# A fused convolution and max pool: moving two of the first loads to ScalarE's DMA queue

## The chip, the core and the metric

The kernel runs on one core of a Trainium2 chip. The core's engines run side by side, each through its own list of instructions: TensorE (PE; its weight loads are listed as PEld), VectorE (DVE), ScalarE (ACT), GpSimd (POOL) and SyncE (SP). Data comes from and goes to the chip's main memory through DMA transfers, which SyncE, ScalarE or GpSimd issue, each on a queue of its own, and which 16 DMA engines carry out. The metric is the time of one execution on the device, in microseconds (us); lower is better.

## The reference

```python
x_pad = np.pad(x, ((0, 0), (0, 0), (pad, pad), (pad, pad)), mode='constant')
conv[b, co] += weight[co, ci, kh, kw] * x_pad[b, ci, kh:kh+h, kw:kw+w]     # over b, co, ci, kh, kw
...
output[b, c, i, j] = np.max(conv[b, c, i*pool_size:(i+1)*pool_size,
                                      j*pool_size:(j+1)*pool_size])
```

`x` is 16 images of 64 channels and 64 x 64 points in f32, `weight` is 128 x 64 x 3 x 3 in f32, and `pool_size` is 2. The output is 16 x 128 x 32 x 32 in f32: a 3 x 3 convolution with a border of zeros, and then the maximum of each 2 x 2 square.

## The kernel before

**Tiles and steps.** Two images of 64 channels fill the 128 partitions, so there are eight pairs of images. Each pair is cut into four chunks of 16 rows of the convolution (eight of the output), which makes 32 steps. A step is of kind K or W (`TYPES`): for K the rows go into TensorE as they are, cast to bf16 (`kx`); for W, sums and differences of neighbouring rows are formed first, from rows kept in f32 (`wx`). The first steps are 0 (K), 1 (W), 2 (K), 3 and 4 (W). `chunk` (L91) says which rows a step needs, `rows_of` (L88) gives them in main memory.

**The first loads (L114 to L129).** In the text of the kernel they stand in this order, all on SyncE's queue: the weights `wraw` (L115, 288 KB), the first nine rows of the first K chunk into `kfirst` (L119, 288 KB), its other eight rows (L120, 256 KB), the second K chunk into `ksecond` (L126, 512 KB), and the first W chunk in two parts (`wload`, L112, 320 KB and 256 KB). All are f32. Later K chunks are loaded by GpSimd's queue, which casts them to bf16 on the way (`kload`, L101); later W chunks by SyncE's queue (L112). Nearly all stores go through SyncE's queue (L485), the last one half through ScalarE's (L487).

**The order of work.** The schedule is written by hand: `ORDER` lists steps by name, and each engine runs its own instructions in that order; a wait is set where data is needed. It begins:

```python
g0 D2 TD2 XOa g2 GS TG0 VD2 D0 XOb XEb TG2 g1 F.0.0 F.0.1 TD0 uG1 GM VG0 GP XEa F.1.0 F.1.1 VD0 F.2.0
uGM EV.0.1 TG1 F.2.1 uGP LB.3 VG2 LK.0.0 TGM X1 LB.4 F.3.0 TGP X2 KS.0 L.11 PA1.2.0 LB.6 Ea F.3.1 VGM
```

- The weights: `g0` (ScalarE, L194), `g1` and `g2` (VectorE, L192) cast the taps, `D2` and `D0` (VectorE, L507 and L508) and `GM` (VectorE, L200) form differences, `GS` and `GP` (GpSimd, L509 and L198) sums. A `T` step turns a block by TensorE (`turn`, L170), a `V` step copies the turned block to where TensorE takes it as weights (`turn_out`; VectorE L188 for D2, D0 and G2, ScalarE L182 and L184 for the others).
- The first K chunk: `XOa`, `XEa` (odd and even rows of the first half of `kfirst`) and `XOb`, `XEb` (the second half) are casts on ScalarE (`cast_rows`, L492). `F.k.0` and `F.k.1` are the products of the two halves (`first_product`, matmuls at L219). F.0 uses the odd rows and the block D2, F.1 the block G0 (`VG0`).
- The second K chunk: `X1` and `X2` cast `ksecond` on ScalarE (`cast_more`, L501).
- `EV` copies a result out on ScalarE (L439), `KS` sums rows on VectorE (L320), `Ea` and `Eb` are row differences of the first W chunk on VectorE (L393).
- `LB.3`, `LB.4`, `LB.6` and so on are later W loads (`late_load`). They wait for the last VectorE step that stands ahead of them in `ORDER`; `L.11` is a W load without that wait. SyncE issues its transfers in order, so a load that waits holds up those behind it.

Before anything is loaded, TensorE runs eight matmuls on ones (L595), and ScalarE loads its table of functions, which is its first instruction and is listed under L194.

Of the kernel before, what the change touches and what calls it, by code (L numbers as in the profile page):

```python
# [11 lines left out]
def kernel(  # L12
# [9 lines left out]
    nc = tc.nc  # L22
# [65 lines left out]
    def rows_of(p, lo, hi):  # L88
        return x[2 * p : 2 * p + 2].rearrange("b c h w -> (b c) h w")[:, lo:hi, :]

    def chunk(q):  # L91
        return (2 * R * q + (q > 0), min(H, 2 * R * (q + 1) + 1))
# [10 lines left out]
    def wload(s, part=None):  # L103
        p, q = place[s]
        lo, hi = chunk(q)
        if s == WSTEPS[0] and q > 0:
            lo = 2 * R * q - 1
        if part == 0:
            hi = 2 * R * q + R + 1
        elif part == 1:  # L110
            lo = 2 * R * q + R + 1
        return nc.sync.dma_start(out=wx[p % NWX][:, lo + 1 : hi + 1, :], in_=rows_of(p, lo, hi))  # L112
# [3 lines left out]
    _, khi = chunk(0)  # L116
    kmid = R + 1
    kfirst = const.tile([128, khi, W], FP32)
    nc.sync.dma_start(out=kfirst[:, 0:kmid, :], in_=rows_of(0, 0, kmid))  # L119
    nc.sync.dma_start(out=kfirst[:, kmid:khi, :], in_=rows_of(0, kmid, khi))  # L120
    klo2, khi2 = chunk(1)
    ksecond = const.tile([128, khi2 - klo2, W], FP32)
    first_loads = (2, 1,)
    for s in first_loads:
        if s == KSTEPS[1]:
            nc.sync.dma_start(out=ksecond, in_=rows_of(0, klo2, khi2))  # L126
        else:
            wload(s, 0)
            wload(s, 1)  # L129
# [508 lines left out]
```

## Time and profile before

| what | value |
|---|---|
| median of 3 runs | 104.94 us (104.35 to 105.64) |
| the profiled execution: its time | 104.47 us |
| the profiled execution: its span | 102.7 us |
| busy: PE, DVE, ACT, POOL | 94%, 89%, 83%, 76% of the span |
| moved by DMA | 23.60 MB, mean 230 GB/s |
| share of the span in the chain that ended last: PE | 88% |
| share of the span in that chain: the load of `kfirst` | 4.2% |

The span runs from the first to the last instruction that the profile shows; the time of the run is 1.8 us longer. Times in the profile count from the start of the span. L12 is line 12 of the kernel. The chain that ended last is followed back from the last instruction, at each step to what released it. "From issue to landing" of a DMA runs from the start of its issue to the last of its completions; each of the 16 DMA engines sends a completion of its own for its eight of the 128 rows of a load. The trace also has every packet that a DMA engine moved, with its queue, start, length and size; here a packet is one partition's row of a load (2304 bytes of `wraw` and of the first half of `kfirst`, 2048 of its second half, 4096 of `ksecond`).

### The profile page before, as it was taken

The numbers are of one execution on the slowest core, as the hardware profiler recorded it, in microseconds if no ns is written. First come the engines' busy times: TensorE is split into PE (matmuls) and PEld (weight loads), VectorE is DVE, ScalarE is ACT, GpSimd is POOL, SyncE is SP. The second block draws the span as 40 slices with busy tenths as digits, with TensorE's granted clock in tenths as the row PEclk, the third lists the DMA queues.
The fourth block names the chain that finished last, engine by engine and source line by source line (L and its number), as shares of the span: only waits on it lengthen the run. The fifth ranks groups of instructions, "written<-read, shape, count | busy, mean of one in ns | idle before, by whom it ended". The sixth has DMA issues, their size and how long they took to land.

```text
span 102.7 us, 2522 instructions
## 1 busy us (share of the span) xinstructions
PE 96.2 (94%) x905; PEld 54.3 (53%) x905; DVE 91.6 (89%) x176; ACT 85.5 (83%) x192; POOL 77.9 (76%) x66
## 2 busy tenths in 40 slices
PE   6969999999999999999999999999999999999920
PEld 2355465444454447655655555567657765555500
DVE  1576979999999999999999989999999999899960
ACT  4278697999889999997998899897989899897830
POOL 6262889995998799489959999789999688990000
PEclk9999999999999999999999999999999999999999
DMA  2989999999999999600538989930803673386553
GB/s 53 286 295 333 281 325 360 362 421 410 293 311 410 311 308 396 220 6 0 175 57 119 245 259 404 389 111 0 307 3 112 216 165 113 106 295 222 208 192 114
DMA packets 13341, 23.60 MB, mean 230 GB/s; under 512 B 1040, under 2 KB 9360, under 8 KB 13328
## 3 DMA queue, kind: packets, MB, share of 16 engines
q1 hardware_dynamic: 12464, 21.20, 58.8%
q0 software_dynamic: 720, 2.10, 11.6%
q8 instruction: 7, 0.11, 0.5%
q10 hardware_dynamic: 144, 0.13, 0.4%
q14 instruction: 6, 0.05, 0.1%
HBM read 17.14 MB, written 8.39 MB: 249 GB/s over the span
## 4 chain that ended last, share of the span: by engine, by line
PE 88%; DMA 4%; DVE 2%; SPq 1%; issue 1%; ACT 0%; DVEq 0%
PE acc L219 86%; DMA kfirst<-in_x_dram 4%; DVE o L477 1%; PE acc L170 1%; DVE acc L467 1%; PE acc L460 1%; SPq L119 0%; ACT kx L492 0%; SPq L115 0%; DVEq L633 0%
## 5 line engine op out<-in xcount | busy, mean ns | idle before, releaser
L219 PEld LDWEIGHTS <-wt 64*128 64x128 bf16 x870 | 51.7, 94 | 39.0 <-issue 2.0
L219 PE MATMUL acc<-wd,wt 64*128 64x504 bf16 (+3 forms) x276 | 54.4, 367 | 0.0
L381 POOL TENSOR_TENSOR wd<-wx 128x1024 bf16<-128x1024 f32 x21 | 49.2, 2360 | 4.5 <-DVE ws L360 2.0
L219 PE MATMUL acc<-kx,wt 64*128 64x504 bf16 (+6 forms) x264 | 44.7, 355 | 0.9 <-DVE wq L508 0.7
L467 DVE TENSOR_TENSOR acc<-acc,ev 128x512 f32<-128x512 f32 x64 | 42.0, 691 | 1.2 <-ACT ev L441 0.7
L219 PE MATMUL acc<-we,wt 64*128 64x512 bf16 (+3 forms) x138 | 32.5, 367 | 0.0
L219 PE MATMUL acc<-ws,wt 64*128 64x512 bf16 (+1 forms) x132 | 32.5, 377 | 0.0
L441 ACT ACTIVATE ev<-acc 128x512 f32<-128x512 f32 x44 | 26.3, 614 | 1.8 <-PE acc L219 1.3
L451 ACT COPY acc<-acc 128x512 f32<-128x512 f32 x42 | 24.5, 591 | 3.0 <-PE acc L219 1.8
L477 DVE TENSOR_TENSOR o<-acc,od 128x256 f32<-128x256 f32 x64 | 24.7, 416 | 0.9 <-ACT od L471 0.9
L471 ACT COPY od<-acc 128x256 f32<-128x256 f32 x64 | 22.8, 382 | 2.2 <-PE acc L219 1.7
L372 POOL TENSOR_TENSOR we<-wx 128x512 bf16<-128x512 f32 x16 | 20.1, 1272 | 4.0 <-PE acc L219 2.4
L219 PE MATMUL acc<-ks,wt 64*128 64x504 bf16 (+1 forms) x60 | 13.7, 377 | 0.0
L439 ACT COPY ev<-acc 128x512 f32<-128x512 f32 x20 | 11.7, 593 | 1.3 <-PE acc L219 1.2
L352 DVE TENSOR_REDUCE ws<-wx 128x512 bf16<-128x1024 f32 x9 | 11.1, 1232 | 0.0
L360 DVE TENSOR_TENSOR ws<-wx 128x512 bf16<-128x512 f32 x7 | 5.3, 766 | 0.0
L320 DVE TENSOR_TENSOR ks<-kx 128x512 bf16<-128x512 bf16 x10 | 4.3, 435 | 0.0
L408 POOL TENSOR_TENSOR wd<-wx 128x512 bf16<-128x512 f32 x2 | 2.5, 1264 | 2.2 <-DVE we L393 2.2
L339 DVE TENSOR_TENSOR ws<-wx,acc 128x512 bf16<-128x512 f32 x6 | 4.1, 675 | 0.0
L595 PE MATMUL acc<-const-bfloat16-1.0 128*128 128x512 bf16 x8 | 3.3, 582 | 0.8 <-PEq L619 0.8
L335 ACT COPY acc<-wx 128x512 f32<-128x512 f32 x6 | 3.6, 598 | 0.1
L372 DVE TENSOR_TENSOR we<-wx 128x512 bf16<-128x512 f32 x4 | 2.9, 749 | 0.3 <-DMA wx<-in_x_dram 0.3
(33 smaller groups left out, 26.6 us busy)
## 6 DMA issues: line engine op xcount, KB each, us to landing
out_dram<-o SPq DMA_DIRECT2D x31, 256.0 KB, 2.9
wx<-in_x_dram SPq DMA_DIRECT2D x10, 512.0 KB, 10.6
wx<-in_x_dram SPq DMA_DIRECT2D x6, 480.0 KB, 9.7
wx<-in_x_dram SPq DMA_DIRECT2D x5, 544.0 KB, 8.5
kx<-in_x_dram POOLq DMA_DIRECT2D x2, 528.0 KB, 7.5
ksecond<-in_x_dram SPq DMA_DIRECT2D x1, 512.0 KB, 6.4
kx<-in_x_dram POOLq DMA_DIRECT2D x1, 496.0 KB, 8.1
wx<-in_x_dram SPq DMA_DIRECT2D x1, 320.0 KB, 6.7
```

Of the source, the lines that this page charges most:

```text
L219: nc.tensor.matmul(acc[t][:, i0:i1, o0:o1], wt[lo : lo + CI, tap_of(m0, kw, h), :], rows(lo, i0, i1, c0, c1), start=start and kw == 1, sto ...
L320: nc.vector.tensor_tensor(out=row["ks", s], in0=t[:, f : f + 2 * R : 2, :], in1=t[:, f + 1 : f + 2 * R : 2, :], op=ADD)
L352: nc.vector.tensor_reduce(out=row["ws", s], in_=t[:, f : f + 2 * R, :].rearrange("p (r two) w -> p r w two", two=2), axis=mybir.AxisListTy ...
L360: nc.vector.tensor_tensor(out=row["ws", s], in0=t[:, f : f + 2 * R : 2, :], in1=t[:, f + 1 : f + 2 * R : 2, :], op=ADD)
L372: inst = (nc.vector if vector else nc.gpsimd).tensor_tensor(out=row["we", s], in0=t[:, f : f + 2 * R : 2, :], in1=t[:, f + 1 : f + 2 * R : ...
L381: nc.gpsimd.tensor_tensor(out=row["wd", s], in0=t[:, f + 1 : f + 1 + 2 * R, :], in1=t[:, f - 1 : f - 1 + 2 * R, :], op=SUB)
L439: nc.scalar.copy(out=ev[s, h], in_=acc[t])
L441: nc.scalar.mul(ev[s, h], acc[t], -1.0)
L451: nc.scalar.copy(out=acc[t], in_=acc[ta[s, h]])
L467: nc.vector.tensor_tensor(out=t, in0=t, in1=ev[s, h], op=MAX)
L471: nc.scalar.copy(out=od[s, h], in_=acc[tb[s, h]][:, :, 1::2])
L477: nc.vector.tensor_tensor(out=ot[s][:, h], in0=acc[t][:, :, 0::2], in1=od[s, h], op=MAX)
```

## The change

Two of the first loads are issued by ScalarE in place of SyncE: the first nine rows of the first K chunk (L119) and the second K chunk (L126). The weights, the rest of the first K chunk (L120) and the first W chunk stay on SyncE's queue.

```diff
     kfirst = const.tile([128, khi, W], FP32)
-    nc.sync.dma_start(out=kfirst[:, 0:kmid, :], in_=rows_of(0, 0, kmid))
+    nc.scalar.dma_start(out=kfirst[:, 0:kmid, :], in_=rows_of(0, 0, kmid))
     nc.sync.dma_start(out=kfirst[:, kmid:khi, :], in_=rows_of(0, kmid, khi))
...
         if s == KSTEPS[1]:
-            nc.sync.dma_start(out=ksecond, in_=rows_of(0, klo2, khi2))
+            nc.scalar.dma_start(out=ksecond, in_=rows_of(0, klo2, khi2))
```

In the lists of instructions that come out, ScalarE issues the two loads first, ahead of its table load; SyncE issues `wraw`, the second half of `kfirst` and the two parts of the first W chunk one after the other. The lists of PE, VectorE and GpSimd are the same in both kernels.

## The prediction

> **What bounds the kernel now.** I read the chain of waits first, because it tells which stretch the end hangs on.
>
> ```profile
> 0.74 0.38 SPq L115
> ...
> 1.18 0.42 SPq L119
> ...
> 1.65 4.30 DMA kfirst<-in_x_dram
> ...
> 5.98 0.41 ACT kx L492
> ...
> 6.43 0.50 PE acc L219 x6
> 6.93 0.33 PE acc L170 x4
> ...
> 12.27 84.18 PE acc L219 x785
> ```
>
> Columns are start, length (us), work. The start hangs on a load: the second half of the first K chunk (L120; call it *b*, the first half L119 *a*) is issued at 1.65 and lands at 5.95; ScalarE casts it (XOb), the second product F.0.1 runs, then TensorE works without a break. The table by stages, cut at the ends of that last row, says whether a late start is made good:
>
> ```profile
> 12.27:96.45 84.18, 84.18 (x794) 48.27 (x795) 81.82 (x154) 76.37 (x172) 71.62 (x42) 1.00 0.72 234
> ```
>
> First PE busy, then PEld, DVE, ACT, POOL, granted clock, DMA share, GB/s. PE is busy 84.18 of 84.18 us: no gap to catch up in. A delay of F.0.1 passes to the end one for one. So the question is when *b* lands. The timeline shows the engines around that:
>
> ```profile
> 3.59 0.53 ACT L194 CAST wq<-wraw 128x192 bf16<-128x192 f32 x1 [1.57 <-DMA wraw<-in_weight_dram]
> ...
> 5.31 0.41 ACT L492 CAST kx<-kfirst 128x256 bf16<-128x256 f32 x1 [1.19 <-DMA kfirst<-in_x_dram]
> ...
> 5.76 0.50 PE L219 MATMUL acc<-kx,wt 64*128 64x256 bf16 x6 [0.70 <-DVE wq L508]
> ...
> 5.98 0.71 ACT L492 CAST kx<-kfirst 128x256 bf16<-128x256 f32 x2 [0.26 <-DMA kfirst<-in_x_dram]
> ...
> 6.43 0.50 PE L219 MATMUL acc<-kx,wt 64*128 64x256 bf16 x6 [0.16 <-ACT kx L492]
> ...
> 8.51 1.14 ACT L501 CAST kx<-ksecond 128x512 bf16<-128x512 f32 x2
> ```
>
> The idle time ahead of a piece and what ended it stand in brackets. By these starts and the loads' completions, weights land at 3.57, *a* at 5.29, *b* at 5.95, ksecond (*ks*) at 8.49 (its cast starts at 8.51). The DMA view of two windows tells how busy the engines are, and how two queues share them:
>
> ```profile
> DMA packets 1103, 2.89 MB, mean 289 GB/s; under 512 B 115, under 2 KB 115, under 8 KB 1103
> ...
> q1 hardware_dynamic: 1101, 2.89, 91.9%
> ```
>
> ```profile
> q1 hardware_dynamic: 84, 0.32, 55.5%
> q0 software_dynamic: 69, 0.14, 48.1%
> ```
>
> The first is 2 to 12 us: SyncE's queue alone holds the 16 engines 92% of the time, so these loads are bound by data, not by issue. The second is 13 to 14.5 us, with a GpSimd load (q0) and SyncE loads (q1) in flight together: packets 69 to 84, time 48% to 55%. Two queues get about equal turns. The packet records of single engines show turns of one packet, mostly q1, q0, q1, q0: the GpSimd load's eight packets on an engine, 0.172 us each (1.4 in all), need about 2.5 us (first packet 11.95, first completion 14.41).
>
> **The change part by part.** *a* and *ks* leave SyncE's queue for ScalarE's; nothing else moves, and the orders on PE, DVE and POOL stay.
>
> SyncE: two issues go. Rows of 0.42 (L119) and 0.43 (L126) with gaps of 0.05 put *b* at 1.18 in place of 1.65 and the two first wx loads at 1.65 and 2.11 in place of 2.59 and 3.05. Value: nothing, because data is the limit; the ends are 0 and 0.47 us of gain for *b*. The Trainium skill, "DMA: Bandwidth & Descriptors", section "Issuing engines are not separate DMA queues", says that issuing from several engines saves only sequencer time, since all share the same 16 engines. By it the gain is at most that 0.47, and the rows agree.
>
> ScalarE: two issues come first, each between 0.37 (its own issue at the end, L487) and 0.70 (GpSimd's, L101). With 0.47 a piece the table load (1.28) moves from 0.74 to 1.68 and ends at 2.96; with 0.70, at 3.42. Both lie ahead of its next work, which waited 1.57 us for the weights until 3.59. Cost 0; the cover is the wait for weights, which here gets longer.
>
> Weights against *a*: a 2304-byte packet takes 0.093 us, and each engine has 8 of each load. Before, the weights went first; now both queues start together and alternate, so the weights end about where *a* ended: all but one engine had finished *a* by 4.45, the last by 5.29. The weights are then late by 0.9 to 1.7. Cover: D2, g2, VD2 and D0 on DVE follow the weights and D0 ended at 5.75, so they end at 6.65 to 7.45; F.0.0 (needs VD2, which ended at 5.08) can start at 6.0 to 6.8. If F.0.1 stayed at 6.43, up to 0.4 of this would show; if *b* is over 1 us late, all is hidden. *a* itself: 0 (the same work is ahead of it).
>
> *b* against *ks*: this is the cost. Before, an engine did weights, *a*, *b*, then *ks*. Now *b* follows the weights in one queue, *ks* follows *a* in the other, and they alternate: 8 packets of 0.084 (0.67 us) between 8 of 0.159 (1.27 us). Ends: at best nothing gets ahead of *b* and its earlier issue counts, -0.47; without any stall, 4.45 + 0.67 + 1.27 = 6.39, +0.44; if *ks* goes wholly first, *b* lands where *ks* did, 8.49, +2.54. I take a value near the last: the work of an engine up to the end of *b* and *ks* together is what it was, stalls included (eleven packets of *ks* took 0.5 to 1.2 us in place of 0.159), and in turns of one the last packet of *b* is one packet of *ks* ahead of the end: 8.49 - 0.16 = 8.33, less about another packet if SyncE's queue has the lead: 8.2. Delay of *b*: 8.2 - 5.95 = 2.25 us.
>
> *ks* ends where it did (8.2 to 8.5). Its casts stand behind EV.0.1, which now starts near 10.3: covered, 0. The first wx loads come behind the same bytes as before: 0; DVE's first wx product at 9.32 served a matmul at 10.91, now near 13.2.
>
> Queued behind XOb on ScalarE: XEb, VG0, XEa, EV.0.1; F.1.0 needs VG0, so F.1.0 goes from 7.22 to 9.5. On SyncE, the late load LB.3 waits for GM on DVE (3.1 us in the waits; GM follows the weights), so it issues 0.9 to 1.7 after 6.6; behind it LB.4 and L.11. LB.3 landed at 13.2 for a DVE difference that TensorE took at 14.83; TensorE is now 2.25 later, so that is covered too. On POOL, the kx load at 7.62 moves as the weights do; its data is needed after 18.
>
> Sum: 0 + 0 + 0 (weights, under *b*) + 2.25 (*b*) = 2.25 us. Profiled execution: span 102.7, its time 104.47, so 104.47 + 2.25 = 106.7. The median of the runs shown, 104.94, is 0.47 above the profiled run; by it the same sum gives 107.2.
>
> **The rivals.** (1) *Turns of a whole load, not of a packet, SyncE first.* Then an engine does weights, *a*, *b*, *ks* as before and the queue change does nothing: 104.5 to 105.2, say 104.7. This is the rival on the other side (not slower); it decides if *b* is served at most one packet of *ks* later. For it: stores of the tail, on both hardware queues, run in stretches of up to eight packets of one queue; against it, those reached the engines at different times, and at 12 to 14 us q1 gave way after single packets. The Trainium skill, same page, section "Queues, rings and completion order", says that an engine round-robins between queue rows a packet at a time, typically 9 to 17 descriptors, which would be all of one load's share of an engine. By that rule the time would be this rival's; the packet records of 13 to 14.5 us speak against it.
>
> (2) *Faster:* *b* lands early behind the weights alone. TensorE's idle times of 0.70 and 0.16 ahead of F.0.0 and F.0.1 are what could go: 104.47 - 0.86 = 103.6. It needs the weights not to be late, and both queues to outrun one; the 92% says there is little room.
>
> (3) *The clock falls.* TensorE would idle from 4.05 to near 8.6 but for 0.8 us of transposes and 0.5 of F.0.0. The warm-up matmuls ran at 3.27/8 = 0.41 us each, half of the later rate (0.215 a start), and full clock is granted from 3.6 us on; if it falls, some 3.3 us of matmuls again run at half rate, +1.7: 108.4. For it, the thinner work; against it, the clock after the last matmul (about 97.8) falls only at 102.6, some 5 us later, and the gap between 5.07 and 5.76 cost nothing. The Trainium skill, "TensorE: Matmul & The Clock Gate", Part 1, puts the fall behind an idle window of about 3.4 us; by it the gap of 1.4 to 2.2 us between F.0.0 and F.0.1 leaves the clock up.
>
> **How the numbers follow.** Turns of one packet, 0.60: 106.7, own range 105.9 to 107.4 (*b* between 7.4 and 8.5 with other stalls, plus the 0.47). Rival 1, 0.20: 104.7. Rival 2, 0.05: 103.6. Rival 3, 0.15: 108.4. The range 104.6 to 108.0 leaves out rival 2, a quarter of rival 1 and two thirds of rival 3: 0.05 + 0.05 + 0.10 = 0.20. Two per cent, about what a measurement of this kernel can tell from no change, is 2.1 us: 107.04 against 104.94. Slower: 0.42 of the first case (0.25) and rival 3 (0.15), 0.40. Faster: 0.03 (most of rival 2 stays under 2%, 102.8). Same: 0.57.
>
> **What would show it.** Right: in the chain the kfirst DMA ends near 8.2, XOb starts there, F.0.1 near 8.6, and PE is then unbroken for the same length; weights land at 4.4 to 5.3; the ACT queue's packets hold about half of the engines from 2 to 8 us. Wrong: kfirst's second half landing before 6.4 (rival 1), PE's matmuls of 8 to 12 us taking twice their length (rival 3), the weights landing after 6 so that D0, not XOb, gates TD0, or a wait inside the stretch of 84 us.

## The result, and the profile after

| | before | changed |
|---|---|---|
| median of 20 runs each | 105.03 us | 106.13 us |
| lowest to highest | 104.26 to 107.18 | 104.94 to 106.61 |
| the profiled execution | 104.47 | 106.61 |
| its span | 102.7 | 104.8 |

The ratio of the changed kernel to the kernel before is 1.0088, with a 95% interval of 1.0059 to 1.0118: slower, by about 0.9%, and within the 2%. Ratios leave out runs over 1.5% above a kernel's fastest; here their records point to TensorE's clock, which is part of the question (below), so medians over all runs stand beside the ratios. The changed kernel's 20 runs fall into two groups, 6 at 104.94 to 105.14 and 14 at 105.97 to 106.61; the profiled run is one of the second.

The chain of waits of the changed kernel (start, length, work):

```profile
0.74 4.37 DMA wraw<-in_weight_dram
...
5.13 0.51 DVE wq L507
...
5.78 0.40 PE acc L170 x4
...
6.20 0.44 DVE wt L188
...
6.68 1.21 PE acc L219 x12
7.89 0.54 PE acc L170 x4
8.43 1.88 PE acc L219 x18
...
14.43 84.19 PE acc L219 x785
```

The chain now starts from the weights, not from `kfirst`: they land at 5.11 in place of 3.57, and D2, its turn, its copy out and the first products follow one another with waits of at most 0.14 us. The long stretch of TensorE is as long as before (84.19 against 84.18 us), and it starts 2.16 us later (14.43 against 12.27). That is the whole loss of the profiled run: 106.61 - 104.47 = 2.14.

The changed kernel's timeline:

```profile
0.74 0.40 ACTq L119 DMA_DIRECT2D kfirst<-in_x_dram  x1
...
1.65 1.28 ACT L194 ACT_TABLE_LOAD   x1 [1.65 <-PEq L619]
...
5.13 0.50 DVE L507 TENSOR_TENSOR wq<-wraw 128x192 bf16<-128x192 f32 x1 [4.00 <-DMA wraw<-in_weight_dram]
...
5.78 0.83 PE L170 MATMUL acc<-ident,wq 128*128 128x128 bf16 x12 [1.61 <-DVE wq L507]
...
6.68 1.21 PE L219 MATMUL acc<-kx,wt 64*128 64x256 bf16 x12
6.68 0.71 ACT L492 CAST kx<-kfirst 128x256 bf16<-128x256 f32 x2 [0.71 <-DMA kfirst<-in_x_dram]
...
8.36 1.94 PE L219 MATMUL acc<-kx,wt 64*128 64x192 bf16 x18
```

The second half of `kfirst` is late too (6.66 against 5.95, where XOb starts at 6.68). F.0.0 and F.0.1 stand in one row of 12 matmuls, which hides a second wait. By the trace's records of single instructions XOb ends at 7.08 and F.0.1 starts at 7.14, the same 0.05 us behind XOb as before (6.38 and 6.43); at the pace of F.0.0, two matmuls each 0.11 us, it could have started at 7.02. So F.0.1 is 0.70 us late by way of *b*, and would have been 0.59 late by the weights alone. TensorE waits 1.61 us for the weights. And the 18 matmuls of F.1 and F.2.0 take 1.94 us. The same 18 before:

```profile
7.22 1.08 PE L219 MATMUL acc<-kx,wt 64*128 64x192 bf16 x18
```

The table by stages of the changed kernel tells why (PE, PEld, DVE, ACT, POOL busy, then granted clock, DMA share, GB/s):

```profile
4.00:6.00 2.00, 0.39 (x6) 0.26 (x6) 0.87 (x2) 0.84 (x2) 0.00 (x0) 1.00 1.00 376
6.00:8.00 2.00, 1.93 (x25) 1.19 (x23) 1.84 (x5) 1.32 (x4) 1.04 (x2) 0.81 0.93 364
8.00:10.00 2.00, 2.00 (x22) 1.36 (x20) 1.53 (x5) 0.54 (x2) 1.86 (x5) 0.50 0.39 108
10.00:12.00 2.00, 2.00 (x25) 1.00 (x21) 0.65 (x2) 1.84 (x5) 0.00 (x0) 0.83 0.96 234
```

From 4 to 6 us TensorE has 0.39 us of work; from 8 to 10 the granted clock is 0.50, where it was 1.00 before. Its records put the half clock at 7.25 to 10.66. PE shows as fully busy there: a matmul at half clock is just longer, so the clock column and the length of one matmul have to be read beside the busy time.

How the two queues share, 1.5 to 6 us:

```profile
q1 hardware_dynamic: 285, 0.56, 46.7%
q10 hardware_dynamic: 237, 0.68, 41.3%
```

Packets, MB, share of the 16 engines: SyncE's queue (q1) and ScalarE's (q10) get about equal turns.

So the theory after the profile: **(weights)** the nine rows of `kfirst` are asked for at the same instant as the weights and no longer behind them, the weights land 1.5 us later, and TensorE starts late; **(clock)** the longer idle time lets the clock fall, or come late, in some runs. Rivals: ksecond's turns ahead of the second half of `kfirst` (the prediction's own step), or a loss from using two queues at all.

### The profile page after: what moved, and what is told of

Same layout as the page of the kernel before. It is cut to its first block, busy times and chain, and to the rows that moved or that the text cites. A ratio compares the mean times of both kernels' runs of the same rounds, so it can differ in the third digit from the quotient of the medians.

```text
span 104.8 us, 2522 instructions
## 1 busy us (share of the span) xinstructions
PE 97.7 (93%) x905; PEld 54.9 (52%) x905; DVE 91.5 (87%) x176; ACT 85.5 (82%) x192; POOL 78.0 (74%) x66
## 4 chain that ended last, share of the span: by engine, by line
PE 88%; DMA 4%; DVE 3%; issue 1%; DVEq 0%
PE acc L219 86%; DMA wraw<-in_weight_dram 4%; PE acc L170 2%; DVE o L477 1%; DVE acc L467 1%; PE acc L460 1%; DVE wq L507 0%; DVE wt L188 0%; DVEq L633 0%
## 5 line engine op out<-in xcount | busy, mean ns | idle before, releaser
L219 PE MATMUL acc<-kx,wt 64*128 64x504 bf16 (+6 forms) x264 | 45.8, 366 | 0.1
L170 PE MATMUL acc<-ident,wq 128*128 128x128 bf16 x25 | 2.6, 244 | 1.6 <-DVE wq L507 1.6
L507 DVE TENSOR_TENSOR wq<-wraw 128x192 bf16<-128x192 f32 x1 | 0.5, 498 | 4.0 <-DMA wraw<-in_weight_dram 4.0
```

The source lines that it names most:

```text
L170: nc.tensor.transpose(tp[:, (j - lo) * CO : (j - lo + 1) * CO], wq[:, j : j + 2, :].rearrange("a b c -> a (b c)"), ident,)
L219: nc.tensor.matmul(acc[t][:, i0:i1, o0:o1], wt[lo : lo + CI, tap_of(m0, kw, h), :], rows(lo, i0, i1, c0, c1), start=start and kw == 1, sto ...
```

## The experiments

Twelve kernels, each timed against the kernel before on the same chip.

| run | median, us | before, same chip | ratio (95% interval) |
|---|---|---|---|
| e1 nine rows alone on ScalarE's queue | 106.22 | 105.03 | 1.0122 (1.0095 to 1.0149) |
| e2 ksecond alone | 106.84 | 105.03 | 1.0178 (1.0151 to 1.0205) |
| e3 changed, 14 warm-up matmuls | 105.16 | 105.03 | 1.0033 (1.0014 to 1.0051) |
| e4 changed, a copy ahead | 105.45 | 105.03 | 1.0051 (1.0030 to 1.0071) |
| e5 before, idle gap filled | 105.27 | 105.23 | 1.0013 (0.9985 to 1.0042) |
| e6 loads wait for the table | 109.92 | 105.23 | 1.0426 (1.0371 to 1.0481) |
| e7 e1 with 14 warm-up matmuls | 105.37 | 105.23 | 1.0029 (0.9997 to 1.0061) |
| e8 one queue, weights second | 105.05 | 105.23 | 1.0037 (0.9999 to 1.0074) |
| e9 e2 with 14 warm-up matmuls | 105.67 | 105.21 | 1.0047 (1.0026 to 1.0068) |
| e10 before, 4 warm-up matmuls | 106.61 | 105.21 | 1.0041 (0.9988 to 1.0094) |
| e11 changed, weights lead by 0.43 us | 104.92 | 105.06 | 1.0003 (0.9987 to 1.0019) |
| e12 e1, weights lead by 0.43 us | 104.74 | 105.06 | 0.9990 (0.9960 to 1.0020) |

**One part of the change alone.** e1 moves L119 only, e2 L126 only.

```diff
-    nc.sync.dma_start(out=kfirst[:, 0:kmid, :], in_=rows_of(0, 0, kmid))
+    nc.scalar.dma_start(out=kfirst[:, 0:kmid, :], in_=rows_of(0, 0, kmid))
```

> Only the first nine rows of kfirst go to ScalarE's queue; ksecond is back on SyncE's, behind the second half of kfirst. Theory (weights): the weights share the engines with those nine rows as in the changed kernel, land near 5.1, and the first product starts at about 6.7 behind them; the time stays at that of the changed kernel, ratio to before 1.007 to 1.013. Rival (ksecond): the delay comes from ksecond getting turns ahead of the second half of kfirst; then that half lands at 6.0 or sooner, and the ratio is 0.997 to 1.003.

In e1 the weights land at 4.58, sooner than the forecast 5.1, and the second half of `kfirst` at 5.63, sooner than before (5.95); yet the ratio is 1.0122. So the loss does not need ksecond ahead of `kfirst`. F.0.0 starts at 6.62, as forecast, but for another reason: full clock came only at 8.98 in this profile, and the 12 transposes ahead of F.0.0 take 1.44 us in place of 0.83.

> Only ksecond goes to ScalarE's queue; weights and both halves of kfirst stay on SyncE's in their old order. Theory (weights): the weights now take turns with ksecond's 4096-byte packets, so they land at 4.5 to 5.2 in place of 3.6, and both halves of kfirst come later too (second half 6.5 to 7.5); ratio 1.005 to 1.015. Rival (the nine rows): only what ScalarE's queue takes ahead of the weights at the very start matters, and ksecond, which is asked for at the same instant, does no harm: ratio 0.997 to 1.003.

In e2 the weights land at 5.24, just past the forecast, and the second half of `kfirst` at 7.13, within it; the ratio, 1.0178, is above the forecast. Whether 4096-byte packets of ksecond delay the weights more than the 2304-byte ones of the nine rows is not shown: 5.24 is later than e1's 4.58, but close to the changed kernel's 5.11. The forecast missed the clock, which in this profile came only at 10.07.

**The clock.** e3 adds six matmuls to the eight of the warm-up.

```diff
-    for n in range(8):
+    for n in (0, 1, 2, 3, 4, 5, 6, 7) + (7,) * 6:
```

> The changed kernel with six more of the 512-column matmuls on ones behind the eight that are there (14 in all); they fill the time in which TensorE waits for the weights. Theory (clock): of the changed kernel's loss in the profiled execution 1.2 us is TensorE at half clock between 7.3 and 10.7, and its runs near 106.2 are those with such a stretch; with TensorE kept busy that stretch goes, nearly all runs fall near 105.0 to 105.3, ratio 0.999 to 1.004. Rival (loads alone): the spread is due to when the loads land; the added matmuls change nothing or cost up to 0.5 us, ratio 1.007 to 1.014.

The weights land at 4.86, hardly sooner than in the changed kernel, but all 12 runs lie at 104.99 to 105.72: the group near 106.2 is gone. e3's chain of waits:

```profile
0.78 5.03 PE acc L595 x14
...
6.55 0.50 PE acc L219 x6
7.05 0.03 issue
7.08 0.51 PE acc L219 x6
...
7.92 1.04 PE acc L219 x18
...
12.92 84.19 PE acc L219 x785
```

The 18 matmuls take 1.04 us again. e7 and e9 do the same to e1 and e2.

> Only the nine first rows on ScalarE's queue, and six more warm-up matmuls (14 in all). Theory (late weights and, through them, the clock): with the clock kept up only the weights' lateness is left, about 1 us of which the first product's old wait for the nine rows hides some; ratio 1.000 to 1.005, and the difference to the same kernel without the six matmuls is over 0.7 us. Rival (loads alone): ratio 1.008 to 1.014, as without them.

> Only ksecond on ScalarE's queue, and six more warm-up matmuls (14 in all). Without them the ratio was 1.0178, with the clock granted only at 10.1 in the profile. Theory (loads and clock, each with its share): the loads land as there (weights near 5.2, second half of kfirst near 7.1), so F.0.1 starts near 7.6 in place of 6.43, and with the full clock granted by 6 the ratio falls to 1.006 to 1.013. Rival (loads alone): it stays at 1.015 to 1.020. Rival (clock alone): 0.999 to 1.004.

e7 fell from 1.0122 to 1.0029 and e9 from 1.0178 to 1.0047, with the loads of e1 and e2 (weights at 4.85 and 5.46). e9 is below the theory's range and its interval reaches into that of the clock alone: about three quarters of e2's loss was the clock, (178 - 47)/178.

What is left in e3 and e9 goes by way of *b* in their profiles. It lands at 6.60 and 7.04, F.0.1 starts 0.05 us behind the end of XOb (at 7.08 and 7.52), and the long stretch starts 0.65 and 1.09 us later than before, as much as *b* is late (5.95 before). In e7 *b* is on time (5.55), and its chain hangs on the 14 warm-up matmuls themselves, which end at 6.40; what is left there is no measure of the loads.

e10 asks the opposite: the kernel before, all its loads as they were, with less warm-up.

```diff
-    for n in range(8):
+    for n in range(4):
```

> The kernel before with four warm-up matmuls in place of eight; loads, queues and all other work as before. Theory (clock): with TensorE idle from 2.5 to 4.2 the full clock is granted a window of 3.4 us later, near 7 to 10, and the matmuls up to then take twice as long: +0.8 to +2.0 us, ratio 1.008 to 1.019, the weights still landing near 3.6. Rival (loads alone): the loads land as before, ratio 0.997 to 1.003.

Eight of its 12 runs are at 106.2 to 108.3, and four at 105.06 to 105.33, as if nothing had been taken away; the median is 1.4 us above that of the kernel before (1.3%, within the forecast, while the ratio, 1.0041, is not). So the clock can cost as much as the change without any load being moved. Its profiled run is no clean case: the weights landed at 3.57, but the two halves of `kfirst` at 6.47 and 7.18. Its timeline shows the matmuls at half speed all the same (the first row is the kernel before, the second e10):

```profile
4.24 0.83 PE L170 MATMUL acc<-ident,wq 128*128 128x128 bf16 x12 [0.19 <-DVE wq L507]
4.24 1.44 PE L170 MATMUL acc<-ident,wq 128*128 128x128 bf16 x12 [1.60 <-DVE wq L507]
```

The clock column says 1.00 there; in this trace its first record is at 10.12, and what lies ahead of the first record counts as full. The length of the matmul is the better witness.

e5 fills the idle 0.7 us of the kernel before with three matmuls behind the transposes (`WU` in `ORDER`, behind TG2).

> The kernel before with three 512-column matmuls on ones more, in TensorE's idle 0.7 us ahead of the first product; loads as before. Theory (clock): some of the kernel's own runs, those of 106.8 to 107.4, are runs in which the full clock was granted late; with the gap filled these go, the median is 104.7 to 105.0, ratio 0.996 to 1.002, and no run is over 106. Rival: such runs have another cause; they stay, and the added matmuls cost up to 0.5 us.

The ratio is that of no change. One of its 12 runs is over 106, and six of 29 of the kernel before on that chip are over 106.5. The mean granted clock that is listed with each run says what such runs are. In the four timings of the kernel before beside these experiments, 20 of 94 runs are over 106, all with a mean of 0.980 or less; the other 74, none over 105.70, have 0.986 or more. So the kernel before has runs with more half clock too. No run of e5 is below 0.988: in favour of the theory, but with 12 runs not enough to call it shown that the filled gap keeps them away.

In the changed kernel two of the 14 runs of the upper group have 0.974, the profiled one among them, and twelve have 0.987 to 1.000. A clock that comes late leaves no mark in that figure: e1's profiled run has 1.000. So in most of these runs the clock probably came late, and the profile shows the rarer case, in which it fell again.

**The weights' lead.** e4 was to hold back ScalarE's loads by a one-column copy ahead of them.

> The changed kernel with a one-column copy on ScalarE ahead of its two loads, so that the table load comes first and the two loads are issued near 2.1 and 2.6 in place of 0.7 and 1.2. Theory (weights): the weights land near 3.6 again, both halves of kfirst by 5.3, the first product starts near 5.6; ratio 0.994 to 1.002. Rival (two queues as such): sharing between the queues slows the start whichever load is ahead; kfirst's halves land after 6.3, ratio 1.004 to 1.015.

It did not: the load was issued at 0.80 beside the table load, which ran from 0.73 to 2.01; ScalarE's queue did not wait for it. The weights land at 5.11, F.0.0 starts at 6.68, both as in the changed kernel. That makes the two profiles a close pair, since here the clock stayed up. e4's stage table:

```profile
6.00:8.00 2.00, 1.93 (x31) 1.36 (x30) 1.84 (x5) 1.42 (x4) 1.03 (x2) 1.00 0.96 381
8.00:10.00 2.00, 2.00 (x32) 1.13 (x30) 1.55 (x5) 1.51 (x4) 2.00 (x5) 1.00 0.50 161
```

Its long stretch starts at 12.99. Against 12.27 before, 0.72 us is what late loads cost in these profiles; from 12.99 to 14.43 in the changed kernel, 1.44 us, is the clock. Why it stayed up is open: TensorE has 1.72 us of work from 3.85 to 7.26 in e4 and the same 1.72 from 3.84 to 7.25 in the changed kernel, and the clock fell only behind the second. Seven of e4's eight runs lie at 105.28 to 105.53, but only six of the 20 of the changed kernel in its lower group, so chance from run to run may not be all of it.

e6 makes the loads wait for a copy into `kfirst` itself, behind the table load.

> The changed kernel, but ScalarE's two loads wait for a one-column copy into kfirst, which ScalarE does behind its table load; they are issued near 2.2 and 2.7 in place of 0.7 and 1.2. Theory (weights): the weights have the engines to themselves and land near 3.6, the first product starts near 5.6, ratio 0.994 to 1.002. Rival (two queues as such): the halves of kfirst land after 6.3 whatever the weights do, ratio 1.004 to 1.015.

The weights land at 3.53, as the theory has it, but the first rows of `kfirst`, issued at 2.25, land only at 9.56. By then SyncE's queue has asked for the second half and the two wx loads. Part of the loss is the clock, which was at half from 7.04 to 13.87. Neither theory foresaw 1.0426: holding the nine rows back by 1.5 us is far too much. Why 288 KB then take 7.3 us is not shown.

e8 needs no second queue: it only exchanges L115 and L119 on SyncE's queue.

> The kernel before, all on SyncE's queue, with two issues exchanged: the nine first rows of kfirst first, the weights second; nothing on ScalarE's queue. Theory (weights): it is the weights' place that costs, whichever queue; they land at 4.3 to 5.2, the first product starts at 5.9 to 6.8, ratio 1.004 to 1.014. Rival (two queues as such): without a second queue nothing is lost, ratio 0.997 to 1.003.

```profile
1.18 3.78 DMA wraw<-in_weight_dram
...
5.62 0.40 PE acc L170 x4
...
6.53 0.83 PE acc L219 x12
...
12.83 84.17 PE acc L219 x785
```

That is the chain of the changed kernel: weights at 4.96, the products of F.0 in one piece behind them, the stretch 0.56 us later than before. Its runs fall into the changed kernel's two groups, eight at 104.95 to 105.09 and four at 106.09 to 106.34. Its ratio, 1.0037 (0.9999 to 1.0074), is at the edge: the place of the weights makes the chain, shown; that it costs time by itself, this run does not settle.

e11 gives the weights a lead of 0.43 us in the changed kernel: VectorE clears four rows of `kfirst` first, and the load waits for that.

```diff
+    nc.vector.memset(kfirst[:, 0:4, :], 0.0)
     nc.scalar.dma_start(out=kfirst[:, 0:kmid, :], in_=rows_of(0, 0, kmid))
```

> The changed kernel, but ScalarE's first load waits for a short clearing of four of its rows by VectorE, so that it is issued near 1.2 in place of 0.74 (as it was in the kernel before); ksecond follows it near 1.65. Theory (weights): with half a microsecond's lead, some five of eight packets on each engine, the weights land at 3.8 to 4.3, the first product starts at 5.5 to 6.0, ratio 0.996 to 1.003. Rival (two queues as such): the weights land after 4.6 all the same, ratio 1.004 to 1.012.

> As the run with the lead, but only the first nine rows on ScalarE's queue and ksecond on SyncE's behind the second half of kfirst. Theory (weights): the weights land at 3.8 to 4.3, the second half of kfirst at 5.4 to 5.8 without stragglers, F.0.1 at 6.0 to 6.3; ratio 0.993 to 1.000, the one arrangement here that could beat both kernels. Rival (two queues as such): 1.004 to 1.012, as without the lead.

e12 does the same with the nine rows alone on ScalarE's queue. In both, the nine rows are issued at 1.17, and the weights land at 3.60 and 3.56, sooner than the 3.8 forecast: 0.43 us bring them back to where they were. Both medians, 104.92 and 104.74, are at the kernel before (105.06 on that chip), and no run of the 24 is over 105.5. The rival "two queues as such" falls: with the old order of issue the second queue costs nothing that these runs can tell.

The rest of e11's start is not restored. Two rows of its timeline:

```profile
3.62 0.53 ACT L195 CAST wq<-wraw 128x192 bf16<-128x192 f32 x1 [0.26 <-DMA wraw<-in_weight_dram]
...
6.67 0.83 PE L220 MATMUL acc<-kx,wt 64*128 64x256 bf16 x12 [1.38 <-ACT kx L493]
```

The halves of `kfirst` land at 6.19 and 6.40, F.0.0 starts at 6.67 and not at 5.5 to 6.0 as forecast, and the long stretch at 12.82, 0.55 late. TensorE idles 1.38 us ahead of F.0.0, nearly as long as in the changed kernel ahead of its transposes, and still has full clock. The place of the gap differs: in e11 the transposes follow the warm-up at once (work from 0.78 to 5.29), in the changed kernel the gap comes behind the warm-up alone (0.78 to 4.16). e12's chain:

```profile
1.17 4.40 DMA kfirst<-in_x_dram
...
6.05 0.83 PE acc L220 x12
...
12.20 84.21 PE acc L220 x785
```

It was the one arrangement that could have beaten both; it beats the changed kernel, and against the kernel before its interval, 0.9960 to 1.0020, includes no change.

## Why the prediction was right or wrong

**Right: the long stretch.** Nothing in it makes good a late start; it was 84.17 to 84.23 us in every profile.

**Right: weights against the nine rows.** Late by 0.9 to 1.7 was forecast; it was 1.54 (5.11 against 3.57). F.0.0 was to start at 6.0 to 6.8 and did at 6.68.

**Right: ScalarE's issues and the table load.** Forecast to 1.68 and 2.96 at 0.47 a piece, seen from 1.65 to 2.93, ahead of the weights.

**Right in its path, wrong in size: the step "*b* against *ks*".** In the profiled run F.0.1 did wait for XOb and so for *b*. But the second half of `kfirst` was to land at 8.2, 2.25 us late; it landed at 6.66, 0.71 late, less than a third of that. The step took the work up to the end of both loads as unchanged, "stalls included". Before, eleven packets of ksecond took over 0.5 us; in the changed kernel not one of its 128 took over 0.25, and ksecond ended at 7.35, not at 8.49. The other half of the step, that the last packet of *b* ends one packet ahead of ksecond's, failed too: it ended 0.7 us ahead. Part of that is that *b* had begun first (its first packet is at 4.28, ksecond's at 4.63).

**Wrong in what it left out: "0 (weights, under *b*)".** As a matter of when F.0.1 can start the cover held, by 0.11 us (7.14 against 7.02). But the term counted only that. Late weights also leave TensorE idle behind its warm-up, and this costs the clock: e1, with *b* landing sooner than before, loses 1.2%, and e11, with the weights on time and both halves of `kfirst` late, loses nothing by its median.

**Wrong in weight: the clock.** Rival 3 had 0.15 and a price of 1.7 us; the price is 1.44 in the pair with e4, but 14 of 20 runs lie in the upper group, whose median is 1.2 us above that of the lower one (106.31 against 105.09). The prediction said that an idle gap of 1.4 to 2.2 us between F.0.0 and F.0.1 would leave the clock up; that gap did not come about, the one that did was 1.61 us ahead of the transposes. For the fall it quoted the Trainium skill, "TensorE: Matmul & The Clock Gate", Part 1, which puts it behind an idle window of some 3.4 us. The windows are there: the clock's records of the changed kernel last 3.413, 3.413 and 92.16 us, the last 27 times 3.413. But a window need not be idle: in the one from 3.84 to 7.25 TensorE did the end of the warm-up (to 4.16), 0.83 us of transposes and part of F.0, 1.72 us in all, and the clock still fell. On this the measurement decides against the page's wording. How much work keeps the clock up is not shown; with e4's 1.72 us it stayed.

**The total.** In the profiled run 2.25 us was forecast and 2.14 measured, 106.7 against 106.61; but as 0.70 for the loads, by which F.0.1 was late, and 1.46 behind it for the clock (0.72 and 1.44 in the pair with e4), not as 2.25 for *b*. The forecast number is right by luck: two errors offset each other. By the medians the loads count for still less. The lower group of the changed kernel (median 105.09) is 0.14 above the median of the 18 runs of the kernel before that lie under 106 (104.95), and with one queue *b* can be late too: in e5's profile, a run of 105.55, it lands at 7.02. So most of the median's rise of 1.1 us is that 14 of 20 runs, in place of two of 20, are over 105.7.

**Rival 1, turns of a whole load.** Against the Trainium skill's typical packet of 9 to 17 descriptors ("DMA: Bandwidth & Descriptors", "Queues, rings and completion order"): the packets of the weights start from 1.75 to 4.57 and those of *a* from 1.97 to 4.76, and the two loads land within 0.2 us of each other (5.11 and 5.29). So the weights did not go ahead as a whole, and here the measurement decides against turns of a load's whole share. How many packets make a turn is not shown, since the packet records do not name the engine.

## What to carry to other kernels

Moving a load to another queue is first of all a change of order: what stood behind the load on the critical path now shares the engines with it, and 0.43 us of lost lead cost 1.5 us in landing. Follow every load whose neighbours change, also the one that the critical path does not go through now. And where TensorE waits at the start, count the idle time also against the clock: in the profile of the changed kernel 1.6 us of idle time behind the warm-up came ahead of a loss of 1.4 us to matmuls at half speed, twice what the late loads cost by themselves. Six more warm-up matmuls (e3), or 0.43 us of lead for the weights (e11), took the late runs away.

## What the runs showed that was not expected

The time of a kernel with a thin start falls into groups, by where the clock's windows of 3.413 us lie against its start: first full clock was recorded at 3.61 before, at 3.84 in the changed kernel, 8.98 in e1, 10.07 in e2 and 4.53 in e3 and e8, and its durations are multiples of 3.413 (98.987 is 29 times). That this phase is chance from run to run was not tested by itself; the groups within one kernel's runs fit it, while e4 and the changed kernel, with nearly the same loads and the same phase in their profiles, have very different shares of late runs.

Stragglers, packets that take several times as long as most of their size, were fewer among ksecond's packets with two queues: over 0.5 us took 11, 9, 2 and 5 of its 128 in the four profiles with one queue (before, e5, e8, e10), and none in the changed kernel, e1, e3, e4, e7, e9, e11 and e12, and one in e2. Among the packets of the weights and *a* this does not hold: 7, 4, 8 and 5 of 256 with one queue, 7 in the changed kernel, none in e11 and 13 in e2. Why is open.
